# Seven block products in place of eight in the feed-forward down products of a two-block model

## The chip, the cores and the metric

The kernel runs on one core of a Trainium2 chip. The metric is the device time of one launch in microseconds, the median of several runs; the profile is one execution taken by the hardware profiler, with its own span.

## The reference, cut to what matters

A residual stream of 256 tokens by 1024 columns goes through two layers of a first block and two of a second. Each layer is a sum of mixers, then a feed-forward part; only that one is touched here.

```python
# first block, width 2816; the convolution runs over tokens, three taps
y = gelu(conv(h @ ffn_w_gate)) * (h @ ffn_w_up)
x = x + rms_norm(y @ ffn_w_down, post_ffn_g)
# second block, width 4096
m = jnp.square(jax.nn.relu(h @ w_up)) @ w_down
x = x + rmsnorm(m, g_post_mlp)
x = x + jax.nn.sigmoid(x @ w_ple_gate) * (p_i @ w_ple_proj)
```

All operands are float32, x is 256 x 1024, and `w_down` is 2816 x 1024 or 4096 x 1024.

## The kernel before

A float32 product is made of three passes of TensorE (`mm3`, L316): each operand is split into a high part (ScalarE copies it to fp32r, which rounds) and the exact rest (VectorE subtracts the high part), and high by high, high by low and low by high are summed in PSUM.

Weights come as a stream of units that is planned ahead in order of use (`plan`, `plan_ffn` at L1219). A unit is 128x1024 numbers: one load on SP's queue into one of three `raw` buffers, one ScalarE copy (L291) to `wh`, one subtraction (L294) to `wl`, the last one by VectorE or, for a few units next to a norm, by GpSimd. `fetch` (L301) emits units up to two ahead of the one in use; a unit in use keeps one of three slots of converted weights. The order of each engine's instructions is set by the framework's scheduler from the order in which they are written and from slots; in the queues it is fixed.

The feed-forward loop (`first_ffn` L1236, second block from L1646) runs over parts of 256 columns of the hidden width. A part has the up product (in the first block gate and up), 48 matmuls of 256 columns each into a bank of PSUM that `pt` gives in turn out of four (`pd`, `pa`); the nonlinearity; the split of its result `y` (128 x 2 x 256: two tiles of hidden columns, 256 tokens) into `f_h` and `f_l`; and the down product, one part behind the up product, in which the tokens are the stationary operand and the weights move: 2 token tiles x 2 row tiles of the weight x 2 column halves of 512 x 3 passes, 24 matmuls into four banks (`acc`, `pc`). The last three parts' down products (`LAST`) come together at the end, one token tile after the other, so that the norm of the first tile can start.

```python
    def downs(p, n):
        return range(n - LAST, n) if p == n else [p - 1] if 0 < p <= n - LAST else []
```

The functions as they are:

Of the kernel before, what the change touches and what calls it, by code (L numbers as in the profile page):

```python
# [47 lines left out]
# steps of the two token tiles between two products  # L48
# [53 lines left out]
# work slots of a group: (tag, bytes of a partition, count), the smallest that fits is taken  # L102
# [7 lines left out]
# work tiles and banks of the mixers of the second block, in phase one and two  # L110
# [8 lines left out]
# banks of PSUM of a group  # L119
# [11 lines left out]
class K:  # L131
    def __init__(self, ctx, tc, a):
# [17 lines left out]
        self.identb = self.cb[:, 0:128]  # L150
        self.hpi = self.cst.tile([128, 1], F, name="hpi")
# [17 lines left out]
    def acc(self):  # L169
        """banks for the products of phase one, in turn"""  # L170
# [18 lines left out]
    def z(self, shape, name, g=None, dt=F, bufs=None):  # L189
        """work tiles of a group of slots"""  # L190
# [16 lines left out]
    def col_load(self, ap, rows, name):  # L207
        """[rows * 128] contiguous values -> [128, rows] (value r * 128 + p at [p, r])."""
# [9 lines left out]
    def rsq(self, ssq, n, mul, add, name="rs"):  # L218
        """(ssq * mul + add) ** -0.5"""
# [15 lines left out]
    def make(self):  # L235
        """the next of what is made once"""
# [5 lines left out]
    def plan(self, key, ap, rows, nk, c0, n):  # L242
        """a block of columns c0..c0 + n, in units of nk tiles of 128 rows"""
# [3 lines left out]
    def tail(self, kind):  # L247
        """the last units planned are followed by a boundary"""
# [4 lines left out]
    def head(self, kind):  # L253
        """the next units may take those slots as well, when what is before the boundary is done"""
# [8 lines left out]
    def convert(self, i, stack):  # L263
        key, ap, r0, nk, c0, n = self.units[i]
        nc = self.nc
        ld = ap.shape[-1]
        raw = self.wp.tile([128, WMAX], F, name="raw", bufs=RAW)
        # the last units of a product before a boundary have slots of their own
# [13 lines left out]
        # next to a boundary the vector engine has the norms to do, and small pieces let those pass  # L282
# [3 lines left out]
        if near and i >= self.near + first:  # L286
            # the norms of the token tiles go ahead
# [28 lines left out]
    def mm3(self, out, a, b, first, last):  # L316
        """out += (ah + al).T @ (bh + bl)"""
# [6 lines left out]
    def tm(self, xT, *blocks, outs=None):  # L324
        """token-major products: each block (key, tiles of rows in a unit, columns) -> its columns of a bank a token tile"""
# [15 lines left out]
    def fm(self, xT, key, out=None):  # L341
        """feature-major product of 256 columns: [128, 2, 256]"""
# [11 lines left out]
    def fm_early(self, xT, key, banks=("acc", "pc"), out=None):  # L354
        """the same by way of a token-major product, which needs one token tile at a time"""
# [18 lines left out]
    def tsplit(self, src, t, hT, lT, k0, nk):  # L374
        """src [128 tokens, nk * 128] -> transposed and split into hT, lT[:, k0:k0 + nk, token tile t]"""
# [14 lines left out]
    def sum_sq(self, a, b, psum=False):  # L390
        """steps: sum of a ** 2 and b ** 2 over 1024 columns, / 1024 + eps, to the power of -1/2"""
# [19 lines left out]
    def warm(self, x, n):  # L411
        """products of no use: the clock of the tensor engine halves when it rests between two products"""
# [1331 lines left out]
```

## Time and profile before

| | us |
|---|---|
| median of three runs | 1549.75 |
| lowest and highest run | 1545.85, 1552.12 |
| span of the profiled execution | 1548.7 |
| median less that span | 1.05 |
| TensorE busy in the span | 1494.2 |
| VectorE busy | 1007.5 |
| ScalarE busy | 827.9 |
| GpSimd busy | 288.0 |

Busy times of engines overlap. TensorE's matmuls are pipelined and their ends modelled, so its pace is read from starts. A name like L294 is the line of the kernel; `wl<-raw,wh` is what is written and what is read.

### The profile page before, as it was taken

What the parts mean: (1) busy time and instruction counts of PE and PEld (TensorE: products, weight loads), DVE (VectorE), ACT (ScalarE), POOL (GpSimd) and SP (SyncE); (2) the same over time, 40 slices, a digit from 0 to 9 for tenths busy, and PEclk for the clock granted to TensorE, in tenths of its full rate; (3) what the DMA queues carried; (4) which work ended last, traced back from release to release, by engine and by line L of the source; (5) the groups of instructions that cost most, each with busy time, mean ns of one, the idle gap of its engine ahead of it and who ended that gap; (6) DMA issues with size and microseconds to landing.
All of it is one profiled execution on the core that took longest, in us unless ns stands there. A gap on an engine that the chain in (4) does not pass through costs nothing.

```text
span 1548.7 us, 25270 instructions
## 1 busy us (share of the span) xinstructions
PE 1494.2 (96%) x9723; PEld 1337.0 (86%) x9731; DVE 1007.5 (65%) x1737; ACT 827.9 (53%) x1443; POOL 288.0 (19%) x377
## 2 busy tenths in 40 slices
PE   7999999999998999999999999999999999999998
PEld 7978889999896887999978888899977888899996
DVE  6897577556789755656666875554566695654455
ACT  5735456445574534544445674555564575555553
POOL 1554210000255322000033122000014231100010
PEclk9999999999999979999999999999999999999999
DMA  7522246666452213666646343556654543466663
GB/s 236 150 84 83 72 149 189 186 183 198 135 158 79 74 57 111 191 188 181 189 135 191 105 138 116 180 187 190 187 188 135 165 124 109 130 190 188 190 194 109
DMA packets 156422, 234.12 MB, mean 151 GB/s; under 512 B 11700, under 2 KB 118158, under 8 KB 156302
## 3 DMA queue, kind: packets, MB, share of 16 engines
q1 hardware_dynamic: 156302, 232.51, 49.5%
q8 instruction: 76, 1.25, 0.3%
q14 instruction: 44, 0.36, 0.1%
HBM read 231.43 MB, written 1.05 MB: 150 GB/s over the span
## 4 chain that ended last, share of the span: by engine, by line
PE 77%; DVE 12%; ACT 4%; DMA 3%; POOL 2%; issue 2%; SPq 0%; ACTq 0%; DVEq 0%; POOLq 0%
PE acc L322 7%; PE acc L320 7%; PE acc L321 7%; PE pa L320 6%; PE pa L322 6%; PE pa L321 6%; PE pc L320 5%; PE pc L322 5%; PE pc L321 5%; PE pd L322 4%; PE pd L321 4%; PE pd L320 4%; DVE wl L294 3%; DVE gl_r L700 1%; ACT wh L291 1%
## 5 line engine op out<-in xcount | busy, mean ns | idle before, releaser
L294 DVE TENSOR_TENSOR wl<-raw,wh 128x1024 fp32r<-128x1024 f32 (+4 forms) x424 | 485.3, 1152 | 362.8 <-ACT wh L291 361.7
L291 ACT ACTIVATE wh<-raw 128x1024 fp32r<-128x1024 f32 (+4 forms) x420 | 433.2, 1035 | 413.2 <-PE pd L321 100.0
L294 POOL TENSOR_TENSOR wl<-raw,wh 128x1024 fp32r<-128x1024 f32 (+1 forms) x26 | 61.7, 2374 | 647.6 <-ACT wh L291 647.6
L322 PE MATMUL pa<-xTh,wl 128*128 128x256 f32 x512 | 145.5, 284 | 0.0
L320 PE MATMUL pa<-xTh,wh 128*128 128x256 f32 x512 | 145.4, 284 | 0.0
L321 PE MATMUL pa<-xTl,wh 128*128 128x256 f32 x512 | 145.2, 284 | 0.0
L322 PE MATMUL pd<-xTh,wl 128*128 128x256 f32 x432 | 122.4, 283 | 0.5 <-DVE wl L294 0.5
L320 PE MATMUL pd<-xTh,wh 128*128 128x256 f32 x432 | 122.3, 283 | 0.0
L321 PE MATMUL pd<-xTl,wh 128*128 128x256 f32 x432 | 122.2, 283 | 0.0
L320 PEld LDWEIGHTS pa<-xTh,wh 128*128 128x128 f32 x512 | 98.2, 192 | 0.3
L321 PEld LDWEIGHTS pa<-xTl,wh 128*128 128x128 f32 x512 | 98.2, 192 | 0.3
L322 PEld LDWEIGHTS pa<-xTh,wl 128*128 128x128 f32 x512 | 98.1, 192 | 0.2
L320 PEld LDWEIGHTS pd<-xTh,wh 128*128 128x128 f32 x432 | 82.8, 192 | 0.9
L321 PEld LDWEIGHTS pd<-xTl,wh 128*128 128x128 f32 x432 | 82.8, 192 | 0.9
L322 PEld LDWEIGHTS pd<-xTh,wl 128*128 128x128 f32 x432 | 82.8, 192 | 0.8 <-DVE wl L294 0.8
L321 PE MATMUL acc<-wl,f_h 128*128 128x512 f32 x200 | 78.4, 392 | 0.0
L322 PE MATMUL acc<-wh,f_l 128*128 128x512 f32 x200 | 77.3, 390 | 0.6 <-DVE f_l L1259 0.6
L321 PE MATMUL pc<-wl,f_h 128*128 128x512 f32 x200 | 77.8, 389 | 0.0
L322 PE MATMUL pc<-wh,f_l 128*128 128x512 f32 x200 | 77.5, 389 | 0.0
L320 PE MATMUL acc<-wh,xTh 128*128 128x512 f32 (+4 forms) x200 | 71.3, 360 | 1.5 <-ACT xTh L477 1.1
L320 PE MATMUL acc<-wh,f_h 128*128 128x512 f32 x200 | 71.4, 393 | 0.2 <-ACT f_h L1257 0.2
L320 PE MATMUL pc<-wh,f_h 128*128 128x512 f32 x200 | 71.3, 389 | 0.0
(630 smaller groups left out, 3869.8 us busy)
## 6 DMA issues: line engine op xcount, KB each, us to landing
raw<-in_w_in_dram SPq DMA_DIRECT2D x84, 512.0 KB, 3.7
raw<-in_w_mlp_up_dram SPq DMA_DIRECT2D x64, 512.0 KB, 3.8
raw<-in_w_mlp_down_dram SPq DMA_DIRECT2D x64, 512.0 KB, 3.7
raw<-in_ffn_w_gate_dram SPq DMA_DIRECT2D x44, 512.0 KB, 3.8
raw<-in_ffn_w_up_dram SPq DMA_DIRECT2D x44, 512.0 KB, 3.8
raw<-in_ffn_w_down_dram SPq DMA_DIRECT2D x44, 512.0 KB, 3.6
raw<-in_w_out_dram SPq DMA_DIRECT2D x32, 512.0 KB, 3.8
raw<-in_w_ple_gate_dram SPq DMA_DIRECT2D x16, 512.0 KB, 4.3
```

The costliest lines, as they stand in the source:

```text
L291: nc.scalar.activation(h[:, p], raw[:, p], AF.Copy)
L294: e.tensor_tensor(l[:, p], raw[:, p], h[:, p].bitcast(F), OP.subtract)
L320: t.matmul(out, ah, bh, start=first, stop=False, skip_group_check=True)
L321: t.matmul(out, ah, bl, start=False, stop=False, skip_group_check=True)
L322: t.matmul(out, al, bh, start=False, stop=last, skip_group_check=True)
L700: nc.vector.tensor_tensor(R[:, j].rearrange("p h (b s) -> p h b s", s=s), ev[:, ft[j], :, 1][:, None].to_broadcast([128, 2, 128 // s, s]), ...
```

## The change

The down product of a part is a product of 2x2 blocks (two token tiles by two row tiles) with 2x2 blocks (two row tiles by two column halves). For all parts but the last three of a loop it is made of seven block products (Winograd's form) in place of eight. Four sums of token blocks and four of weight blocks are made by GpSimd, each of the operands is then split into high and low part, and the seven products are summed over all these parts in seven banks of PSUM. After the loop the seven banks are combined on ScalarE and VectorE, split once more, and added into the four banks of the last three parts by matmuls with the identity. The eighth bank is all that is left to the up products. In the plan, four units of seven products (two, one, two and two blocks of 128x512) take the place of two units of 128x1024; the loads are the same. They use three slots of their own (`th`, `tl`). In the first block the gate product is copied from PSUM first, and half of the seven products stand between gate and up product. The tables that are made once move from the third part to the last.

Comments removed by the diff and unchanged lines are left out.

```diff
+        self.identr = self.cst.tile([128, 128], FR, name="identr")
+        nc.scalar.activation(self.identr, self.ident, AF.Copy)
...
     def convert(self, i, stack):
+        if nk is None:
+            return self.convert_seven(i, key, ap, r0, c0)
...
     def plan_ffn(self, ups, down, l, width):
-                for key, w in ups:
+                for j, (key, w) in enumerate(ups):
                     self.plan((key, l, p), w, D, 4, p * 256, 256)
-            for q in self.downs(p, n):
-                self.plan((down[0], l, q), down[1][q * 256:q * 256 + 256], 256, 1, 0, D)
+                    for q in self.sevens(p, n):
+                        for which in self.share(j, len(ups)):
+                            self.tails.add(len(self.units))
+                            self.units.append(((down[0], l, q, "s", which), down[1], q * 256, None, which, 0))
+            else:
+                for q in range(n - LAST, n):
+                    self.plan((down[0], l, q), down[1][q * 256:q * 256 + 256], 256, 1, 0, D)
...
+    def sevens(p, n):
+        return [p - 1] if 0 < p <= n - LAST else []
+    def share(j, n):
+        return range(4 * j // n, 4 * (j + 1) // n)
+    def convert_seven(self, i, key, ap, r0, which):
+        nc = self.nc
+        if which == 0:
+            b = []
+            for j in range(2):
+                raw = self.wp.tile([128, WMAX], F, name="raw", bufs=RAW)
+                nc.sync.dma_start(raw, ap[r0 + j * 128:r0 + j * 128 + 128])
+                b += [raw[:, :512], raw[:, 512:]]
+            b11, b12, b21, b22 = b
+            t1, t2, t3, t4 = (self.z([128, 512], "f_t", "d") for _ in range(4))
+            e = nc.gpsimd
+            e.tensor_tensor(t1, b12, b11, OP.subtract)
+            e.tensor_tensor(t3, b22, b12, OP.subtract)
+            e.tensor_tensor(t2, b22, t1, OP.subtract)
+            e.tensor_tensor(t4, b21, t2, OP.subtract)
+            self.sb = [(b11, b21), (b22,), (t1, t3), (t2, t4)]
+        src = self.sb[which]
+        h = self.wp.tile([128, D], FR, name="wh", tag="th", bufs=TAIL)
+        l = self.wp.tile([128, D], FR, name="wl", tag="tl", bufs=TAIL)
+        h, l = (x.rearrange("p (k n) -> p k n", n=512) for x in (h, l))
+        for j, x in enumerate(src):
+            nc.scalar.activation(h[:, j], x, AF.Copy)
+            nc.vector.tensor_tensor(l[:, j], x, h[:, j].bitcast(F), OP.subtract)
+        self.made[i] = (h, l)
+    def seven_banks(self):
+        b = self.bank
+        p2, p3 = b("acc"), b("acc")
+        p4 = b("pc")
+        p1, p5 = b("pd"), b("pd")
+        p6, p7 = b("pa"), b("pa")
+        return [None, p1, p2, p3, p4, p5, p6, p7]
+    def seven_tokens(self, y):
+        nc = self.nc
+        a = self.z([128, 4, 128], "f_s", "G")
+        a11, a12, a21, a22 = y[:, 0, :128], y[:, 1, :128], y[:, 0, 128:], y[:, 1, 128:]
+        e = nc.gpsimd
+        e.tensor_tensor(a[:, 0], a21, a22, OP.add)
+        e.tensor_tensor(a[:, 1], a[:, 0], a11, OP.subtract)
+        e.tensor_tensor(a[:, 2], a11, a21, OP.subtract)
+        e.tensor_tensor(a[:, 3], a12, a[:, 1], OP.subtract)
+        ah, al = (self.z([128, 3, 128], n, g, dt=FR) for n, g in (("f_h", "c"), ("f_l", "a")))
+        sh, sl = (self.z([128, 4, 128], n, "G", dt=FR) for n in ("f_sh", "f_sl"))
+        for h, l, x in ((ah[:, :2], al[:, :2], y[:, :, :128]), (ah[:, 2], al[:, 2], a22), (sh, sl, a)):
+            nc.scalar.activation(h, x, AF.Copy)
+            nc.vector.tensor_tensor(l, x, h.bitcast(F), OP.subtract)
+        pair = lambda h, l, j: (h[:, j], l[:, j])
+        A = lambda j: pair(ah, al, j)
+        S = lambda j: pair(sh, sl, j)
+        return [((1, A(0)), (2, A(1))), ((3, S(3)),), ((5, S(0)), (7, S(2))), ((6, S(1)), (4, A(2)))]
+    def seven(self, P, ops, key, whichs, first, last):
+        for which in whichs:
+            h, l = self.unit(key + ("s", which))
+            for j, (p, a) in enumerate(ops[which]):
+                self.mm3(P[p], a, (h[:, j], l[:, j]), first, last and p in (1, 5, 6, 7))
+    def seven_sums(self, P):
+        nc = self.nc
+        z = lambda: self.z([128, 512], "f_u", "d")
+        c11, u, c21, c12, c22 = z(), z(), z(), z(), z()
+        nc.scalar.activation(c11, P[1], AF.Copy)
+        nc.vector.tensor_tensor(u, c11, P[6], OP.add)
+        nc.vector.tensor_tensor(c21, u, P[7], OP.add)
+        nc.vector.tensor_tensor(c12, u, P[5], OP.add)
+        nc.vector.tensor_tensor(c22, c21, P[5], OP.add)
+        out = []
+        for x in (c11, c12, c21, c22):
...
+            nc.scalar.activation(h, x, AF.Copy)
+            nc.gpsimd.tensor_tensor(l, x, h.bitcast(F), OP.subtract)
+            out.append((h, l))
+        return out
+    def seven_end(self, P, sums):
+        accs = [P[2], P[3], P[4], self.bank("pc")]
+        for i, (b, (h, l)) in enumerate(zip(accs, sums)):
+            self.nc.tensor.matmul(b, self.identr, h, start=i == 3, stop=False, skip_group_check=True)
+            self.nc.tensor.matmul(b, self.identr, l, start=False, stop=False, skip_group_check=True)
+        return [accs[:2], accs[2:]]
+    def up_bank(self, p, n):
+        return self.bank("pc") if p < n - LAST + 2 else self.pt()
     def first_ffn(self, l, xT):
...
-                pg = self.fm(xT, ("gate", l, p), self.pt()) if p else self.fm_early(xT, ("gate", l, p))
+                pg = self.fm(xT, ("gate", l, p), self.up_bank(p, np_)) if p else self.fm_early(xT, ("gate", l, p))
+                x = self.z([128, 2, 256], "f_g", "c")
+                nc.scalar.activation(x, pg, AF.Copy)
...
-                        nc.vector.scalar_tensor_tensor(c[:, f, d:], pg[:, f, :256 - d], w(2 - d, f), c[:, f, d:],
+                        nc.vector.scalar_tensor_tensor(c[:, f, d:], x[:, f, :256 - d], w(2 - d, f), c[:, f, d:],
...
+                if p == 1:
+                    P = self.seven_banks()
+                for q in qs:
+                    self.seven(P, g[q], ("down", l, q), self.share(0, 2), q == 0, q == np_ - LAST - 1)
...
+                if p < np_ - LAST:
+                    g[p] = self.seven_tokens(y)
...
+                for q in qs:
+                    self.seven(P, g[q], ("down", l, q), self.share(1, 2), q == 0, q == np_ - LAST - 1)
+                    del g[q]
+            if p == np_ - LAST:
+                sums = self.seven_sums(P)
+            if p == np_ - 1:
                 self.make()
...
+        accs = self.seven_end(P, sums)
```

The loop of the second block is changed in the same way, with all four units of a part behind the up product.

## Rows read from the trace of the kernel before

**Rows 1.** The page: span, then busy time, share of the span and instructions.
```profile
span 1548.7 us, 25270 instructions
PE 1494.2 (96%) x9723; PEld 1337.0 (86%) x9731; DVE 1007.5 (65%) x1737; ACT 827.9 (53%) x1443; POOL 288.0 (19%) x377
```

**Rows 2.** Windows: stretch, its length, busy time of each engine, granted clock, DMA.
```profile
core 0: us, PE busy (x) PEld busy (x) DVE busy (x) ACT busy (x) POOL busy (x), PEclk, DMA share, GB/s
275.00:350.00 75.00, 75.00 (x541) 71.16 (x540) 45.91 (x55) 35.33 (x44) 0.53 (x1) 1.00 0.63 188
1025.00:1125.00 100.00, 100.00 (x657) 92.05 (x656) 50.21 (x45) 54.44 (x64) 0.00 (x0) 1.00 0.61 190
```

**Rows 3.** Timeline of TensorE, second block: start, duration, engine, line, operation.
```profile
1022.12 0.28 PE L320 MATMUL pd<-xTh,wh 128*128 128x256 f32 x1
...
1027.88 0.40 PE L320 MATMUL acc<-wh,f_h 128*128 128x512 f32 x1
...
1033.34 0.28 PE L320 MATMUL pa<-xTh,wh 128*128 128x256 f32 x1
```

**Rows 4.** Timeline of SP's queue, first block: two successive gate loads.
```profile
276.07 3.21 SPq L281 DMA_DIRECT2D raw<-in_ffn_w_gate_dram  x2
...
293.05 3.21 SPq L281 DMA_DIRECT2D raw<-in_ffn_w_gate_dram  x2
```

**Rows 5.** Timeline of VectorE: back-to-back pairs, and three convolution steps.
```profile
596.56 1.29 DVE L294 TENSOR_TENSOR wl<-raw,wh 128x512 fp32r<-128x512 f32 x2 [6.18 <-ACT wh L291]
...
186.78 2.36 DVE L294 TENSOR_TENSOR wl<-raw,wh 128x1024 fp32r<-128x1024 f32 x2 [2.77 <-ACT wh L291]
...
261.81 1.38 DVE L1250 SCALAR_TENSOR_TENSOR f_c<-pd,f_cw,f_c 128x255 f32<-128x255 f32 x3
```

**Rows 6.** Timeline of GpSimd at three places.
```profile
1132.15 4.76 POOL L294 TENSOR_TENSOR wl<-raw,wh 128x1024 fp32r<-128x1024 f32 x2 [170.38 <-ACT wh L291]
...
386.83 1.39 POOL L294 TENSOR_TENSOR wl<-raw,wh 128x560 fp32r<-128x560 f32 x1 [0.20 <-ACT wh L291]
...
147.71 0.46 POOL L962 TENSOR_TENSOR c_q<-c_q,rp 128x128 f32<-128x128 f32 x1 [0.83 <-DVE rp L961]
```

**Rows 7.** Timeline of GpSimd, then of VectorE, from 204.5 to 209.
```profile
205.71 2.40 POOL L294 TENSOR_TENSOR wl<-raw,wh 128x1024 fp32r<-128x1024 f32 x1 [2.63 <-ACT wh L291]
...
204.66 0.74 DVE L451 SCALAR_TENSOR_TENSOR x<-ny,rs,x 128x512 f32<-128x512 f32 x1
205.32 0.68 DVE L479 TENSOR_TENSOR xTl<-pd,xTh 128x512 fp32r<-128x512 f32 x1
205.92 2.73 DVE L451 SCALAR_TENSOR_TENSOR x<-ny,rs,x 128x512 f32<-128x512 f32 x1
```

**Rows 8.** Timeline of GpSimd, then of VectorE, from 66.7 to 69.7.
```profile
66.71 0.74 POOL L854 TENSOR_TENSOR a_g<-a_g,ngain 128x256 f32<-128x256 f32 x1
67.40 1.45 POOL L704 TENSOR_TENSOR gl_e<-gl_e,b_k 128x128 f32<-128x128 f32 x1
68.81 0.80 POOL L1059 TENSOR_TENSOR d_kd<-d_qk,d_eb 128x256 f32<-128x256 f32 x1
...
67.01 1.52 DVE L294 TENSOR_TENSOR wl<-raw,wh 128x1024 fp32r<-128x1024 f32 x1
68.45 0.68 DVE L1056 TENSOR_TENSOR d_kb<-d_qk,d_beta 128x256 f32<-128x256 f32 x1
```

**Rows 9.** Timeline of ScalarE in the second block's loop.
```profile
1030.20 0.63 ACT L1656 ACTIVATE f_h<-f_y 128x512 fp32r<-128x512 f32 x1
1030.82 1.06 ACT L291 ACTIVATE wh<-raw 128x1024 fp32r<-128x1024 f32 x1
```

**Rows 10.** The page's DMA issues: operation, count, KB each, us to landing.
```profile
raw<-in_w_mlp_down_dram SPq DMA_DIRECT2D x64, 512.0 KB, 3.7
```

**Rows 11.** Timeline of TensorE at a norm; in brackets the idle time before.
```profile
800.01 1.73 PE L472 MATMUL pd<-cf,nxn 128*128 128x128 f32 x8 [2.43 <-DVE nxn L469]
```

**Rows 12.** Windows, the same columns as in rows 2.
```profile
802.00:804.00 2.00, 2.00 (x5) 1.62 (x5) 2.00 (x4) 1.95 (x4) 0.60 (x1) 0.50 0.00 0
```

More of the change, by code (lines that the diff above doesn't have):

```diff
@@ L1231, in downs @@
     @staticmethod
-    def downs(p, n):
-        return range(n - LAST, n) if p == n else [p - 1] if 0 < p <= n - LAST else []
+    def sevens(p, n):
+        return [p - 1] if 0 < p <= n - LAST else []
+    @staticmethod
+    def share(j, n):
[24 more added lines that the diff above has]
+        self.made[i] = (h, l)
@@ new lines, in seven @@
+    def seven(self, P, ops, key, whichs, first, last):
[14 more added lines that the diff above has]
+        for x in (c11, c12, c21, c22):
+            h, l = (self.z([128, 512], n, "G", dt=FR) if n == "f_vh" else self.z([128, 512], n, "N", dt=FR) for n in ("f_vh", "f_vl"))
+            nc.scalar.activation(h, x, AF.Copy)
+            nc.gpsimd.tensor_tensor(l, x, h.bitcast(F), OP.subtract)
+            out.append((h, l))
+        return out
@@ L1241, in first_ffn @@
         for p in range(np_ + 1):
+            qs = self.sevens(p, np_)
             if p < np_:
-                pg = self.fm(xT, ("gate", l, p), self.pt()) if p else self.fm_early(xT, ("gate", l, p))
+                pg = self.fm(xT, ("gate", l, p), self.up_bank(p, np_)) if p else self.fm_early(xT, ("gate", l, p))
+                x = self.z([128, 2, 256], "f_g", "c")
+                nc.scalar.activation(x, pg, AF.Copy)
                 c = self.z([128, 2, 256], "f_c", "c")
@@ L1246, in first_ffn @@
                 for f in range(2):
-                    nc.scalar.activation(c[:, f], pg[:, f], AF.Copy, scale=w(2, f))
+                    nc.scalar.activation(c[:, f], x[:, f], AF.Copy, scale=w(2, f))
                 for f in range(2):
                     for d in (1, 2):
-                        nc.vector.scalar_tensor_tensor(c[:, f, d:], pg[:, f, :256 - d], w(2 - d, f), c[:, f, d:],
+                        nc.vector.scalar_tensor_tensor(c[:, f, d:], x[:, f, :256 - d], w(2 - d, f), c[:, f, d:],
@@ L1251, in first_ffn @@
                                                        op0=OP.mult, op1=OP.add)
                 nc.scalar.activation(c, c, AF.Gelu_apprx_tanh)
-                pu = self.fm(xT, ("up", l, p), self.pt()) if p else self.fm_early(xT, ("up", l, p))
+                if p == 1:
+                    P = self.seven_banks()
+                for q in qs:
+                    self.seven(P, g[q], ("down", l, q), self.share(0, 2), q == 0, q == np_ - LAST - 1)
+                pu = self.fm(xT, ("up", l, p), self.up_bank(p, np_)) if p else self.fm_early(xT, ("up", l, p))
@@ L1265, in first_ffn @@
-            qs = self.downs(p, np_)
-            if qs:
-                self.down(accs, [(g[q][0][:, k], g[q][1][:, k], ("down", l, q, k)) for q in qs for k in range(2)],
-                          p == 1, p == np_)
-            for q in qs:
-                del g[q]
+                if p < np_ - LAST:
+                    g[p] = self.seven_tokens(y)
+                else:
+                    gh = self.z([128, 2, 256], "f_h", "c", dt=FR)
+                    nc.scalar.activation(gh, y, AF.Copy)
+                    gl = self.z([128, 2, 256], "f_l", "a", dt=FR)
+                    nc.vector.tensor_tensor(gl, y, gh.bitcast(F), OP.subtract)
+                    g[p] = (gh, gl)
@@ L1271, in first_ffn @@
+                for q in qs:
[4 more added lines that the diff above has]
+            if p == np_ - 1:
+                self.make()
+        accs = self.seven_end(P, sums)
+        self.down(accs, [(g[q][0][:, k], g[q][1][:, k], ("down", l, q, k)) for q in range(np_ - LAST, np_) for k in range(2)],
+                  False, True)
         return accs
@@ L1647, in second_layer @@
         g, pp = {}, None
-        for p in range(np_ + 1):
-            if p < np_:
-                pu = self.fm(xT, ("2up", l, p), self.pt()) if p > 1 else self.fm_early(xT, ("2up", l, p))
-                r = self.z([128, 2, 256], "f_c", "c")
-                nc.scalar.activation(r, pu, AF.Relu)
-                y = self.z([128, 2, 256], "f_y", "a")
-                nc.scalar.activation(y, r, AF.Square)
+        for p in range(np_):
+            pu = self.fm(xT, ("2up", l, p), self.up_bank(p, np_)) if p > 1 else self.fm_early(xT, ("2up", l, p))
+            r = self.z([128, 2, 256], "f_c", "c")
+            nc.scalar.activation(r, pu, AF.Relu)
+            y = self.z([128, 2, 256], "f_y", "a")
+            nc.scalar.activation(y, r, AF.Square)
+            if p < np_ - LAST:
+                g[p] = self.seven_tokens(y)
+            else:
                 gh = self.z([128, 2, 256], "f_h", "c", dt=FR)
@@ L1660, in second_layer @@
             if p == 1:
-                accs = self.acc4()
-            qs = self.downs(p, np_)
-            if qs:
-                self.down(accs, [(g[q][0][:, k], g[q][1][:, k], ("2down", l, q, k)) for q in qs for k in range(2)],
-                          p == 1, p == np_)
-            for q in qs:
-                del g[q]
+                P = self.seven_banks()
+            for q in self.sevens(p, np_):
+                self.seven(P, g[q], ("2down", l, q), self.share(0, 1), q == 0, q == np_ - LAST - 1)
+                del g[q]
+            if p == np_ - LAST:
+                sums = self.seven_sums(P)
+        accs = self.seven_end(P, sums)
+        self.down(accs, [(g[q][0][:, k], g[q][1][:, k], ("2down", l, q, k)) for q in range(np_ - LAST, np_) for k in range(2)],
+                  False, True)
         ws = [self.unit(("2pp", l, k)) for k in range(2)]
```

8 lines of the change are left out of this document (removed).

## Prediction

> **What bounds the kernel now.** I read the page first: of a span of 1548.7 us TensorE is busy in 1494.2, while GpSimd has only 288.0 us of work [rows 1]. Then the table by windows, for one stretch inside the feed-forward loop of each block: TensorE is busy for the whole of both, at full granted clock, ScalarE and VectorE for about half to six tenths, and GpSimd for nothing but a crumb [rows 2]. The reader is to see that in these loops TensorE alone sets the pace and that GpSimd's queue is empty. The page calls a matmul busy until its modelled end, so the pace is read from starts in the timeline: in the second block one part of the loop starts at 1022.12 and the next at 1033.34, a period of 11.22 us [rows 3]. It holds 48 products of 256 columns (the up product, 1022.12 to 1027.88, so 0.120 us each) and 24 of 512 columns (the down product, 1027.88 to 1033.34, 5.46 us, so 0.2275 us each) and no gap. In the first block the loads come round every 16.98 us [rows 4], that is two up-like products and one down product (2 x 5.76 + 5.46 = 16.98): no gap either.
>
> **What the change takes from TensorE.** A part's down product is eight block products of three passes, 24 matmuls; seven make 21. So 3 x 0.2275 = 0.68 us go in each part that is changed: 8 parts in each of two layers of the first block and 13 in each of two of the second, 42 in all, 126 matmuls, 28.7 us. Added are 8 matmuls with the identity at the end of each of four loops, 32 x 0.2275 = 7.3 us, behind products that keep TensorE busy. Alone this is -21.4 us, and a part would take 10.54 us in the second block and 16.30 in the first.
>
> **What it adds elsewhere.** Per changed part, for the weights: the two halves of a down weight were two tiles of 1024 columns, copied and subtracted in one piece each; now seven blocks of 512 columns are, after four subtractions of 128x512 on GpSimd (t1 to t4). For the tokens: 896 columns are split in three pieces in place of 512 in one, after four GpSimd operations of 128x128. In the first block the gate product is also copied out of PSUM by ScalarE (one copy of 128x512), since the loop has one bank for it now; its four convolution steps then read SBUF only.
>
> VectorE, from pairs that ran back to back [rows 5]: 1.29 / 2 = 0.645 us for 512 columns, 2.36 / 2 = 1.18 for 1024, hence 1.045 ns a column and, on that line, 0.38 for 256 and 0.24 for 128. A part of the second block: 2 x 1.18 (up weights) + 7 x 0.645 + (0.645 + 0.38 + 0.24) = 8.14 us. The first block: 4 x 1.18 + 4.515 + 1.265 + four convolution steps at 0.46 [rows 5] = 12.34 us, and one product with PSUM beside it, 0.65.
>
> GpSimd [rows 6]: 4.76 / 2 = 2.38 us for 1024 columns and 1.39 for 560, 2.13 ns a column, so about 1.29 for 512; 0.46 for 128. Four and four: 5.16 + 1.84 = 7.00 us a part, in loops where it had nothing.
>
> ScalarE in the second block: 0.63 us for a 512-column copy, 1.06 for 1024 [rows 9]; 2 x 1.06 + 7 x 0.63 + 1.2 (relu and square, at that price) + some 1.3 for the tokens = about 9 us, under the 10.54; in the first block 4 x 1.06 + 4.41 + 1.3 and four more at 0.63, 12.5 us under 16.30. Each engine taken by itself fits.
>
> **The pair that doesn't fit.** The rows at 205 us show VectorE and GpSimd side by side [rows 7]. The same VectorE step that takes 0.74 us took 2.73 when it came 0.21 us behind a GpSimd subtraction: it ended at 208.65, 0.54 after GpSimd's end at 208.11, and 0.54 is its 512 columns at 1.045 ns. It had waited for the whole of it. The step between, with an operand in PSUM, took its usual 0.68 although it ended inside the GpSimd instruction. So what excludes GpSimd is VectorE reading two operands of SBUF. Every subtraction raw minus high part does that, and so, after the change, does each convolution step. The two engines then have one budget, and behind a blocked subtraction stand, in VectorE's in-order queue, those of the next up weights, whose low parts TensorE's second or third pass reads.
>
> The sum of durations: 8.14 + 7.00 = 15.14 us in the second block against a period of 11.22; 12.34 + 7.00 = 19.34 in the first against 16.98. The lower bound is that only the columns exclude each other: 6528 x 1.045 + 2560 x 2.13 = 12.28 us in the second block, and 9594 x 1.045 + 5.45 = 15.48 in the first, where TensorE's 16.30 would bind.
>
> Rows 8 put a price between: five operations in turn on the two engines, from 66.71 to 69.61, 2.90 us [rows 8]. By the prices for one (0.74, 1.18, 0.46, 0.38, 0.74) they sum to 3.50, by columns alone to 2.71. Where both queues are full, then, the pair needs 0.83 of the sum: 12.6 us.
>
> The Trainium skill, SBUF — State Buffer, section "Who interferes with whom", has this as a rule: a VectorE instruction with two SBUF inputs and a GpSimd one that reads SBUF contend, and the second to issue is blocked until the first is done. By that rule as it stands, with whole durations and no idle time, the kernel would take about 1549 + 26 x 3.92 + 16 x 2.36 + 7 = 1696 us; by the proportion of rows 8 it would be 1549 + 26 x 1.38 - 16 x 0.68 + 7 = 1581.
>
> I take 15.14 for the second block: a saturated 12.6 needs both queues full, and each VectorE subtraction waits for its own ScalarE copy, each t for a landed load and for the t before it. For the first block I take the middle between TensorE's 16.30 and 19.34, 17.8: its loop has 6 us more, and its 0.65 us product with PSUM leaves the pair free.
>
> **What is near the path besides.** Loads: two of three raw buffers stay taken until the t chain is through. A load lands 3.7 us after issue [rows 10]; 2 x (3.7 + 2.3) for the up weights, an estimated 8 and 12 for the two halves of a down weight (the landing and two or four steps of the t chain), 32 us over three buffers, 10.7 a part: under 15, so not the bound, but every other load queues in order on SP behind it. Banks: up products have one bank; the next up product starts 21 matmuls later (4.8 us; 9 or 12, 2 us or more, in the first block), and the one ScalarE or VectorE read in between, about 0.63 us, is hidden by that. The sums (five ScalarE copies, four VectorE sums and four GpSimd subtractions, 5.2 us on GpSimd) lie under two up products without a down product, 11.5 us; uncovered they would cost 2 us a loop. The one-time tables move to the last up part: nothing, or 2 us once. Identity tile: one copy at the start, nothing.
>
> **Sum.** 26 x (15.14 - 11.22) = +102; 16 x (17.8 - 16.98) = +13; identity products +7; the second block's loops begin with converted units in hand and end without new ones, so half a part's excess less at each of four ends, -8. Together +114: 1549 + 114, about 1663. The page's span is 1 us below the median 1549.75 of the runs, which I use as the start: 1664.
>
> **Rivals.**
> 1. Forecast: the pair of VectorE and GpSimd sets the loop; 1620 to 1710, 1664 likeliest. Chance 0.60.
> 2. The pair interleaves as densely as it can, and only the second block suffers: 26 x 1.06 - 16 x 0.68 + 7 = +24, 1574. For it: rows 8. Against: those five operations were all ready. Chance 0.17.
> 3. Waits come on top of the budget. A unit of seven products has three converted slots for four units, so the fourth unit's copies start when the first unit's products end, with 9 matmuls (2.05 us) of cover; two copies and two subtractions (2 x 0.65 + 2 x 0.645), with a GpSimd instruction of 1.29 let in before each subtraction, are about 4.5 us: 2.5 us bare in each of 42 parts, +105, about 1770. TensorE's clock points the same way: after a gap of 2.43 us [rows 11] it was at 0.50 [rows 12], the 1.2 GHz level. Against: bare time is partly time that the pair uses. Chance 0.15.
> 4. The other side: the pair hides, because GpSimd's instructions fall into VectorE's idle half and are short enough to be let in; TensorE stays the bound and the matmuls saved are the result: 1549.75 - 21.4 = 1528. It decides if the pair's need falls under 10.54 us a part. Rows 7 and 8 speak against: even columns alone ask 12.28. Chance 0.06. Between this and rival 2, no change: 0.02.
>
> **Range and chances.** Low is rival 2, high is rival 3: 1574 to 1770, which leaves out rival 4 and about half of the outer two. A measurement of this kernel can tell 0.5%, 8 us. Faster 0.06, same 0.03, slower 0.91.
>
> **What would show it.** In the profile after: periods of the second block's loop near 15 us (10.5 if rival 4 holds, 12.3 if rival 2) and of the first near 17.8; GpSimd busy near 7 us of each part; VectorE subtractions of 512 columns with a mean well over 0.645 us; TensorE waiting for `wl` of the seven, or for the token parts, in every part; TensorE's busy share in these loops near 0.7 in the second block. I am wrong if the loops hold no TensorE waits although GpSimd works, or if the waits end on loads or PSUM banks instead.

## The result and the profile after

The kernel with seven products takes 1695.88 us (median of four runs, 1689.69 to 1698.44) beside 1550.21 for the kernel before on the same chip: 1.0941 times as long, with an interval of 1.0907 to 1.0975. The profiled execution has a span of 1687.9 us, 139.2 more than that of before.

The page of the changed kernel: span, busy times, the engines' shares of the chain that ended last, and four groups of instructions.

```profile
span 1687.9 us, 26284 instructions
PE 1529.8 (91%) x9637; PEld 1346.7 (80%) x9637; DVE 1325.3 (79%) x2043; ACT 938.9 (56%) x1779; POOL 716.5 (42%) x729
...
PE 43%; DVE 23%; DMA 11%; ACT 9%; issue 7%; POOL 7%; SPq 0%; ACTq 0%; POOLq 0%; DVEq 0%
...
L1278 DVE TENSOR_TENSOR wl<-f_t,wh 128x512 fp32r<-128x512 f32 x168 | 148.3, 912 | 11.5 <-ACT wh L1277 11.5
L1278 DVE TENSOR_TENSOR wl<-raw,wh 128x512 fp32r<-128x512 f32 x126 | 146.0, 1188 | 5.2 <-ACT wh L1277 5.2
...
L1267 POOL TENSOR_TENSOR f_t<-raw 128x512 f32<-128x512 f32 x42 | 65.0, 1547 | 185.9 <-DMA raw<-in_w_mlp_down_dram 79.7
```

GpSimd has gone from 288.0 to 716.5 us, VectorE from 1007.5 to 1325.3 [rows 1]. The shares of the chain before were these:

```profile
PE 77%; DVE 12%; ACT 4%; DMA 3%; POOL 2%; issue 2%; SPq 0%; ACTq 0%; DVEq 0%; POOLq 0%
```

So TensorE's share has fallen from 77% to 43%, and VectorE's has risen from 12% to 23%. The subtraction of 512 columns, 0.645 us where VectorE is alone [rows 5], has a mean of 0.912 or 1.188 here, and a GpSimd sum of 512 columns 1.547 in place of 1.29 [rows 6]. Both are longer where they stand beside each other (experiments 1 and 8).

The windows of before in the same places [rows 2], after (busy time of each engine with its count, then granted clock and load):

```profile
245.00:385.00 140.00, 121.83 (x791) 113.80 (x790) 117.22 (x130) 74.67 (x121) 58.54 (x51) 0.91 0.48 151
1060.00:1200.00 140.00, 122.54 (x733) 104.15 (x732) 134.17 (x125) 81.11 (x144) 103.86 (x84) 0.98 0.49 155
```

In the second block (second row) VectorE is at work, or blocked, for 134.17 of 140 us, so it sets the pace there. In the first block it isn't full, and the granted clock is 0.91. The periods, from SP's queue: two loads of the second block's up weights, two of the first block's gate weights.

```profile
1109.49 6.58 SPq L285 DMA_DIRECT2D raw<-in_w_mlp_up_dram  x2
1122.99 6.56 SPq L285 DMA_DIRECT2D raw<-in_w_mlp_up_dram  x2
...
285.16 2.10 SPq L285 DMA_DIRECT2D raw<-in_ffn_w_gate_dram  x2
305.69 2.10 SPq L285 DMA_DIRECT2D raw<-in_ffn_w_gate_dram  x2
```

One part takes 13.5 us in the second block (11.22 before [rows 3]) and 20.5 in the first (16.98 [rows 4]). Some of TensorE's longest waits (total, times, longest):

```profile
PE pc L324 <- DVE f_y L1372: 35.2, 12, 6.1
PE pc L325 <- DVE wl L1278: 34.6, 23, 2.5
...
PE pa L476 <- DVE nxn L473: 12.5, 6, 6.5
```

The row that is left out, for `nxn` into `pd`, is 14.3 us here and 15.3 before. The second row is the wait that the prediction named, for the low part of a seven's weights. Here is one of them in the second block's timeline (start, duration, engine, line, idle time before and its releaser):

```profile
1151.39 1.40 POOL L1268 TENSOR_TENSOR f_t<-raw 128x512 f32<-128x512 f32 x1 [0.30 <-DMA raw<-in_w_mlp_down_dram]
1151.56 2.79 DVE L1303 TENSOR_TENSOR f_l<-f_y,f_h 128x256 fp32r<-128x256 f32 x2
...
1152.75 1.45 POOL L1269 TENSOR_TENSOR f_t<-raw,f_t 128x512 f32<-128x512 f32 x1
...
1154.28 0.94 DVE L1278 TENSOR_TENSOR wl<-f_t,wh 128x512 fp32r<-128x512 f32 x1
...
1155.14 2.64 DVE L1278 TENSOR_TENSOR wl<-raw,wh 128x512 fp32r<-128x512 f32 x2
1155.27 0.50 PE L325 MATMUL pc<-wl,f_h 128*128 128x512 f32 x1 [1.91 <-DVE wl L1278]
1155.50 1.74 POOL L1270 TENSOR_TENSOR f_t<-raw,f_t 128x512 f32<-128x512 f32 x1
```

Two token splits, of 256 and of 128 columns (the row gives the form of the first), took 2.79 us, 0.63 in experiment 1, while GpSimd ran two weight sums. The low part of a seven's weights was queued behind them (1154.28), and TensorE stood 1.91 us for it. The Trainium skill, SBUF — State Buffer, section "Who interferes with whom", says that of such a pair the second to issue waits; these rows agree.

The wait in the first row was not in the prediction. It is the first block's, and the line is the product `f_y` that empties the only bank of the up products:

```profile
321.25 1.47 POOL L1269 TENSOR_TENSOR f_t<-raw,f_t 128x512 f32<-128x512 f32 x1
321.49 3.48 DVE L1278 TENSOR_TENSOR wl<-raw,wh 128x512 fp32r<-128x512 f32 x2
322.80 1.62 POOL L1270 TENSOR_TENSOR f_t<-raw,f_t 128x512 f32<-128x512 f32 x1
322.83 0.40 PE L324 MATMUL pa<-wh,f_sh 128*128 128x512 f32 x1
...
324.00 0.39 PE L326 MATMUL pc<-wh,f_l 128*128 128x512 f32 x1
...
324.89 1.21 DVE L298 TENSOR_TENSOR wl<-raw,wh 128x1024 fp32r<-128x1024 f32 x1
326.03 0.68 DVE L1372 TENSOR_TENSOR f_y<-f_c,pc 128x512 f32<-128x512 f32 x1
...
326.76 0.39 PE L324 MATMUL pc<-xTh,wh 128*128 128x256 f32 x1 [2.37 <-DVE f_y L1372]
```

Read it upward: TensorE stood 2.37 us for `f_y`, which ran for its usual 0.68; it was queued behind three subtractions, the first two of which took 3.48 us in place of 1.29 beside two GpSimd sums. Between the up product and the next gate product TensorE has only six matmuls, from 322.83 to 324.00: the scheduler has put five of the seven products, 15 matmuls, between gate and up product, where the kernel's text has half of them. After the same gap one part earlier the clock fell to the 1.2 GHz level (the column behind POOL is the granted clock; TensorE had idled from 303.86 to 306.31 and then been busy without a break):

```profile
305.00:306.00 1.00, 0.00 (x0) 0.00 (x0) 1.00 (x2) 0.29 (x1) 0.00 (x0) 1.00 0.14 37
...
309.00:310.00 1.00, 1.00 (x6) 1.00 (x6) 1.00 (x2) 0.32 (x1) 0.65 (x1) 0.50 1.05 362
311.00:312.00 1.00, 1.00 (x11) 1.00 (x10) 0.27 (x2) 0.73 (x1) 0.00 (x0) 1.00 0.09 30
```

From 307.5 to 310.9 matmuls of 256 columns started 0.214 us apart in place of 0.120, which costs 1.5 us. So 16.30 of products, 2.4 of gap and 1.5 of half clock make 20.2 of the 20.5.

The wait for `nxn` into `pa` (3.0 us in all before) is at the norm before the second block's feed-forward part, where the weight sums of the first part already run:

```profile
1018.33 1.74 POOL L1267 TENSOR_TENSOR f_t<-raw 128x512 f32<-128x512 f32 x1
1018.84 3.46 DVE L1278 TENSOR_TENSOR wl<-raw,wh 128x512 fp32r<-128x512 f32 x2
...
1022.22 1.75 DVE L408 SCALAR_TENSOR_TENSOR nsc<-x 128x512 f32<-128x512 f32 x1
...
1027.49 0.90 PE L476 MATMUL pa<-cf,nxn 128*128 128x128 f32 x3 [6.51 <-DVE nxn L473]
```

**Where the 139 us are.** From the first read of a norm (`nsc<-acc`) to the first of the norm behind, the four feed-forward stages took 192.0, 195.7, 189.6 and 189.4 us before and take 229.0, 225.2, 226.8 and 229.4: +37.0, +29.5, +37.2 and +40.0, together 143.7. All else is 4.5 shorter; one stretch of mixers alone is 9 shorter, which has another cause (last section). Eight parts of the first block at +3.5 us (20.5 less 16.98) and the stage's eight identity products (1.8) make 29.8 of its stages; thirteen parts of the second at +2.27 (13.49 less 11.22) and 1.8 make 31.3. What is left over, 7.2, -0.3, 5.9 and 8.7 us, lies at the starts and ends of the loops.

### The profile page after: what moved, and what is told of

Read it like the earlier page. It is cut to its first block, busy times and chain, and to the rows that moved or that the text cites. A ratio compares the mean times of both kernels' runs of the same rounds, so it can differ in the third digit from the quotient of the medians.

```text
span 1687.9 us, 26284 instructions
## 1 busy us (share of the span) xinstructions
PE 1529.8 (91%) x9637; PEld 1346.7 (80%) x9637; DVE 1325.3 (79%) x2043; ACT 938.9 (56%) x1779; POOL 716.5 (42%) x729
## 4 chain that ended last, share of the span: by engine, by line
PE 43%; DVE 23%; DMA 11%; ACT 9%; issue 7%; POOL 7%; SPq 0%; ACTq 0%; POOLq 0%; DVEq 0%
DVE wl L1278 6%; DVE wl L298 6%; PE pc L324 5%; PE pc L325 5%; PE pc L326 5%; PE acc L326 4%; ACT wh L295 3%; PE acc L324 3%; PE acc L325 3%; DMA raw<-in_ffn_w_down_dram 3%; PE pa L324 2%; PE pa L325 2%; PE pa L326 2%; DMA raw<-in_ffn_w_up_dram 2%; DMA raw<-in_w_mlp_up_dram 2%
## 5 line engine op out<-in xcount | busy, mean ns | idle before, releaser
L298 DVE TENSOR_TENSOR wl<-raw,wh 128x1024 fp32r<-128x1024 f32 (+5 forms) x336 | 400.2, 1200 | 177.0 <-ACT wh L295 172.9
L295 ACT ACTIVATE wh<-raw 128x1024 fp32r<-128x1024 f32 (+3 forms) x336 | 343.2, 1026 | 231.9 <-DMA raw<-in_w_mlp_up_dram 43.2
L324 PE MATMUL pc<-xTh,wh 128*128 128x256 f32 x784 | 236.4, 301 | 36.9 <-DVE f_y L1372 35.2
L326 PE MATMUL pc<-xTh,wl 128*128 128x256 f32 x784 | 234.1, 299 | 6.7 <-DVE wl L298 6.7
L325 PE MATMUL pc<-xTl,wh 128*128 128x256 f32 x784 | 234.0, 298 | 0.0
L324 PEld LDWEIGHTS pc<-xTh,wh 128*128 128x128 f32 x784 | 162.5, 207 | 45.7 <-DVE f_y L1372 40.9
L326 PEld LDWEIGHTS pc<-xTh,wl 128*128 128x128 f32 x784 | 162.7, 207 | 8.9 <-DVE wl L298 7.2
L325 PEld LDWEIGHTS pc<-xTl,wh 128*128 128x128 f32 x784 | 163.0, 208 | 2.1
L1278 DVE TENSOR_TENSOR wl<-f_t,wh 128x512 fp32r<-128x512 f32 x168 | 148.3, 912 | 11.5 <-ACT wh L1277 11.5
L1278 DVE TENSOR_TENSOR wl<-raw,wh 128x512 fp32r<-128x512 f32 x126 | 146.0, 1188 | 5.2 <-ACT wh L1277 5.2
```

The lines of the kernel that those rows point to most:

```text
L295: nc.scalar.activation(h[:, p], raw[:, p], AF.Copy)
L298: e.tensor_tensor(l[:, p], raw[:, p], h[:, p].bitcast(F), OP.subtract)
L324: t.matmul(out, ah, bh, start=first, stop=False, skip_group_check=True)
L325: t.matmul(out, ah, bl, start=False, stop=False, skip_group_check=True)
L326: t.matmul(out, al, bh, start=False, stop=last, skip_group_check=True)
L1278: nc.vector.tensor_tensor(l[:, j], x, h[:, j].bitcast(F), OP.subtract)
```

## Experiments

Theory A: VectorE's steps with two operands in SBUF and GpSimd's sums exclude each other. Theory B: the form of the product costs the time by itself (three slots for four units, one bank, later tokens), whoever makes the sums. Ratios are to the kernel before on the same chip.

**1. The same instruction slots, but next to nothing read.** Each weight sum becomes two memsets of 0.525 us and a subtraction of two columns, together about its duration; a token sum becomes one memset and such a subtraction. The sums themselves are left out, so that the products are of other numbers.

```diff
+def write_only(e, out, x, y, op):
+    for _ in range(2 if out.shape[-1] == 512 else 1):
+        e.memset(out, 0.0)
+    e.tensor_tensor(out[:, :2], x[:, :2], y[:, :2], op)
...
-            e.tensor_tensor(t1, b12, b11, OP.subtract)
+            write_only(e, t1, b12, b11, OP.subtract)
...
```

> Each of the eight GpSimd sums of a part is replaced by writing only: one or two memsets of its tile (about as long) and a subtraction of two columns, so that it still waits for the same loads; the sums themselves are left out. Theory A (VectorE's subtractions with two operands in SBUF and GpSimd's reading sums exclude each other): the 512-column subtractions fall back to a mean of 0.65 to 0.70 us, the period of the second block's loop falls from 13.49 us to 10.6 to 11.2, that of the first block's from 20.48 to 16.3 to 17.5, and the time is 1535 to 1580 us. Theory B (the order of the queues, the three raw buffers held by the chain of four sums, and the single PSUM bank of the up products set the periods, whatever GpSimd reads): the periods stay within 1 us of 13.5 and 20.5, and the time is above 1660.

Measured: 1552.41 us, 1.0033 (1.0005 to 1.006). Its page, and its up loads in the second block:

```profile
PE 1485.0 (95%) x9637; PEld 1321.3 (85%) x9637; DVE 1123.8 (72%) x2043; ACT 935.7 (60%) x1779; POOL 612.7 (39%) x1233
...
L1284 DVE TENSOR_TENSOR wl<-raw,wh 128x512 fp32r<-128x512 f32 x126 | 83.0, 686 | 15.9 <-ACT wh L1283 15.6
...
1059.91 3.78 SPq L291 DMA_DIRECT2D raw<-in_w_mlp_up_dram  x2
1070.47 3.80 SPq L291 DMA_DIRECT2D raw<-in_w_mlp_up_dram  x2
1081.25 3.80 SPq L291 DMA_DIRECT2D raw<-in_w_mlp_up_dram  x2
```

GpSimd is busy for 612.7 us, not far from 716.5, yet the subtraction is back at 0.686 and the period at 10.7 us (10.54 predicted for TensorE alone); in the first block it is 16.8 on average (gate loads at 260.13 and 327.17, four parts; 16.30 predicted). So some 144 us of the loss come from what GpSimd reads, and slots and bank by themselves cost 0.1 to 0.5 us a part: theory A. That it isn't the other numbers is shown by experiment 2, where they are right and the subtractions as short. Experiment 1 also shows that the saving is real inside the loops and yet worth nothing over the whole: the time is that of before, where the matmuls saved less the identity products ask for 21.4 us less. Part of where it goes is seen at the start of the second block's loop, in TensorE's timeline of this kernel:

```profile
967.89 1.78 PE L482 MATMUL pa<-cf,nxn 128*128 128x128 f32 x8 [2.28 <-DVE nxn L479]
...
979.81 0.50 PE L330 MATMUL pd<-wh,f_h 128*128 128x512 f32 x1 [2.19 <-ACT f_h L1308]
...
984.34 0.50 PE L330 MATMUL pc<-wh,f_h 128*128 128x512 f32 x1 [2.87 <-ACT wh L1283]
```

7.3 us of waits, where the kernel before has none longer than 0.8 in the same stage. The second token tile of the norm comes later (2.28; why is not shown), and the first seven products come before ScalarE has split the first tokens and copied the second weight unit (2.19 and 2.87). With contention these last two places wait 2.20 and 2.67.

**2. All sums on VectorE.**

```diff
-            e = nc.gpsimd
+            e = nc.vector
...
-        e = nc.gpsimd
+        e = nc.vector
```

> All eight sums of a part go from GpSimd to VectorE, nothing is left out. Theory A: no contention is left, VectorE alone has 8.14 + 4 x 0.645 + 4 x 0.24 = 11.7 us a part in the second block and 12.99 + 3.54 = 16.5 in the first, so the periods are 11.7 to 12.3 and 16.5 to 17.5 and the time is 1560 to 1605 us. Theory B: VectorE's fixed queue only grows longer, what it frees (bank, raw buffers) comes later, and the time is that of the changed kernel or more, 1690 to 1740.

Measured: 1593.66, 1.0283 (1.0237 to 1.0328). Periods of 11.4 us in the second block (1085.83 to 1131.44, four parts) and 17.4 in the first; the subtractions are at 0.69 to 0.70. The same sums cost 102 us less where they add 3.5 us a part to an engine that is already more than half full. Without contention VectorE's own need sets the second block: 8.14 + 4 x 0.645 + 4 x 0.24 = 11.7, a little over what it took.

**3. First block: the bank emptied by ScalarE**, so that the next product needn't wait for VectorE's queue.

```diff
-                nc.vector.tensor_tensor(y, c, pu, OP.mult)
+                nc.scalar.activation(y, pu, AF.Copy)
+                nc.vector.tensor_tensor(y, c, y, OP.mult)
```

> In the first block ScalarE copies the up product out of its bank as soon as it is done, and VectorE multiplies from SBUF; the rest is the changed kernel. Theory C (the first block's 4 us a part over TensorE's 16.30 are the wait for the one bank, 2.4 us, and the half clock that follows it, 1.6 us): the waits of the gate product for the multiplication go, the granted clock in the loop returns to 1.00, the period falls to 17 to 18.5 and the time to 1645 to 1670 us. Theory A alone (the pair's budget sets the first block's period as well): the period stays above 19.5, the waits turn up at converted weights, and the time stays within 15 us of 1696.

Measured: 1678.51, 1.0836 (1.0791 to 1.0882), between the two. The first block's period is 19.3 us (20.5), and the clock over four of its parts 0.96 (0.91). One wait of it, and what stands before it:

```profile
336.22 3.44 DVE L1278 TENSOR_TENSOR wl<-raw,wh 128x512 fp32r<-128x512 f32 x2
336.39 0.63 ACT L1365 ACTIVATE f_c<-f_c 128x512 f32<-128x512 f32 x1 [0.84 <-DVE f_c L1363]
...
337.88 0.58 ACT L1372 ACTIVATE f_y<-pc 128x512 f32<-128x512 f32 x1
...
338.51 0.39 PE L324 MATMUL pc<-xTh,wh 128*128 128x256 f32 x1 [2.08 <-ACT f_y L1372]
```

TensorE now waits for ScalarE's copy, that stands behind the gelu in ScalarE's queue, and the gelu waited for the convolution that GpSimd had held up on VectorE (1.51 us for one step of 0.46). The delay reaches the bank on either road; the emptying by VectorE was one place where it showed. Of the 1.2 us a part that were won, some 1.0 belong to the clock, by an estimate: 0.96 in place of 0.91 over some 20 us.

**4. Seven products in the second block only**, the first block as before.

```diff
-        self.plan_ffn((("gate", a["ffn_w_gate"][l]), ...
+        self.plan_eight((("gate", a["ffn_w_gate"][l]), ...
...
```

> Seven products in the second block only; the first block's loop is that of the kernel before. If the losses are local to each loop, as the profile's stage lengths say (first block +37 and +30 us, second block +37 and +40), the time is 1550 + 77 + about 4 = 1620 to 1640 us, with the second block's period unchanged at 13.5 and the first block's back at 16.98. If the second block inherits part of its loss from the first (load stream, clock), it is below 1610.

Measured: 1626.05, 1.0492 (1.042 to 1.0564). The periods are 16.98 and 13.49, each as in the kernel that it is from; about 78 us of the loss are the second block's and 70 the first's.

**5. The first part's weight sums held behind the norm** in front of the loop.

```diff
...
+                if key[2] == 0:
+                    for ins in self.gates.get("pool", ()):
+                        stack.enter_context(self.tc.issue_after(ins))
...
```

> The changed kernel, but the weight sums of each loop's first part on GpSimd are queued behind the last power of the norm ahead of the loop. Theory A says that in the changed kernel these sums, which are ready early, block VectorE's norm steps at the second block's loops (TensorE waits 6.5 us for the second token tile there, 0.7 us in the kernel before). Then that wait falls to 0.7 to 3.9 us and the time by 5 to 14 us, to 1682 to 1691. Rival: the start of the loop is late for its loads and for token parts converted late; then the wait moves to them and the time stays within 4 us of 1696.

Measured: 1692.15, 1.0937 (1.0902 to 1.0971), not to be told from 1.0941. The longest wait for `nxn` on that line falls from 6.5 to 3.3 us, and all waits for it in that stage, the third, from 6.5 to 4.3. The stage is 1.9 us shorter (the four are 227.6, 225.0, 224.9 and 229.7): that is what the hold is worth at most, and too little to show in the whole time.

**6. Weight sums on VectorE, token sums on GpSimd.**

```diff
             t1, t2, t3, t4 = (self.z([128, 512], "f_t", "d") for _ in range(4))
-            e = nc.gpsimd
+            e = nc.vector
```

> The four weight sums of a part on VectorE, the four token sums (128x128) left on GpSimd; nothing is left out. If the price is the columns that GpSimd reads, only a fifth of them is left, VectorE has 10.7 us a part in the second block and 15.6 in the first, and the kernel lies between writing only and all sums on VectorE: 1560 to 1594 us, periods 10.9 to 11.8 and 16.5 to 17.4. If what counts is that GpSimd works at all between the products (a wait of VectorE and ScalarE for its results), it is slower than all sums on VectorE, 1600 to 1650.

Measured: 1613.45, 1.0443 (1.0409 to 1.0476): 20 us more than with all sums on VectorE. The main expectation was less; the time lies in the range of the other one, 1600 to 1650. The second block has the same period (11.4), the first a longer one (18.4 beside 17.4), and `f_y` is waited for again:

```profile
PE pc L324 <- DVE f_y L1372: 21.1, 13, 4.0
```

Two rows of the second block show that short GpSimd sums are not let in for nothing either; a VectorE step of 512 columns is at 0.68 where GpSimd is idle:

```profile
1068.96 0.90 POOL L1296 TENSOR_TENSOR f_s<-f_s,f_y 128x128 f32<-128x128 f32 x1
...
1069.48 0.94 DVE L1268 TENSOR_TENSOR f_t<-raw 128x512 f32<-128x512 f32 x1
```

Why the first block lost a whole microsecond is not shown: before the `f_y` at 300.04 and at 318.62 GpSimd had been idle for over 14 us, so there it can't have held up VectorE's queue, and between 301 and 307 the granted clock was 0.72.

**7. Weight sums made twice on GpSimd.**

```diff
+            e.tensor_tensor(t1, b12, b11, OP.subtract)
+            e.tensor_tensor(t3, b22, b12, OP.subtract)
+            e.tensor_tensor(t2, b22, t1, OP.subtract)
+            e.tensor_tensor(t4, b21, t2, OP.subtract)
```

> The changed kernel with the four weight sums of a part computed twice on GpSimd, 5.16 us more of reading a part; nothing is left out. Theory A: the pair is the bound, so each part grows by 0.83 to 1.0 of that, 4.3 to 5.2 us, and the time by 42 x 4.3 to 42 x 5.2 us, to 1875 to 1915. Rival: GpSimd's idle time in the loops (a fourth in the second block, half in the first) takes most of it: under 1780.

Measured: 1832.2, 1.1854 (1.1787 to 1.1921), 136 us more than with the sums once, between the expectations. The second block's period is 17.5 us (up loads from 1142.20 to 1212.11, four parts), the first's 23.1. Four more sums cost 4.0 and 2.6 us: 1.0 us each in the second block, 0.77 of their 1.29. The granted clock from 1142 to 1212 is 0.85, but VectorE is busy for 65.95 and GpSimd for 67.00 of these 70 us, so it is the pair that sets the pace. With both queues full, then, a part takes 17.5 of the 20.3 us that its durations sum to, 0.86.

**8. The kernel before with seven idle GpSimd additions** of 128x512 in each part of the second block, read by nobody.

```diff
+                for _ in range(7):
+                    u = self.z([128, 2, 256], "f_u", "d")
+                    nc.gpsimd.tensor_tensor(u, y, y, OP.add)
```

> The kernel before, with seven additions of 128x512 on GpSimd in each part of the second block's loop (9.0 us, both operands the part's own activations, the results unused). Nothing waits for them and TensorE's work is that of before. Theory A: VectorE's subtractions (5.4 us a part) and these exclude each other, 12.4 us a part by columns and 14.4 by durations against a period of 11.22; the loop's period becomes 12.0 to 14.4 and the time 1575 to 1650 us. Rival: without a dependence it stays hidden, 1545 to 1556 us.

Measured: 1568.03, 1.0141 (1.0106 to 1.0176), between the expectations. Groups of its page, and a wait of TensorE:

```profile
L294 DVE TENSOR_TENSOR wl<-raw,wh 128x1024 fp32r<-128x1024 f32 (+4 forms) x424 | 545.8, 1296 | 310.9 <-ACT wh L291 309.4
...
L1657 POOL TENSOR_TENSOR f_u<-f_y 128x512 f32<-128x512 f32 x224 | 354.0, 1616 | 20.6 <-ACT f_y L1654 20.6
...
PE pd L321 <- POOL wl L294: 11.0, 2, 5.5
```

The period is 11.37 us (loads at 1029.98, 1041.34, 1052.71). GpSimd is never idle in the loop, each addition takes 1.62 in place of 1.29, and VectorE's subtractions of 1024 columns 1.2 to 2.1 in place of 1.18; but they are ready early, and TensorE hardly notices. 11.0 of the 22 us are two waits at the loops' ends for a low part that GpSimd itself makes and that stands behind its backlog. By columns alone, one engine after the other, the pair would need 4608 x 1.045 + 3584 x 2.13 ns = 12.4 us a part, and it did all of it in 11.37: the sum of columns, which the prediction took for a lower bound, isn't one. A GpSimd addition kept VectorE from at most (11.37 - 4.82) / 7 = 0.94 us.

**9 and 10. The one-time tables** made behind the first up part of the first loop in place of the last, in the changed kernel and in that of experiment 1.

```diff
-            if p == np_ - 1:
+            if p == 0:
                 self.make()
```

> The changed kernel, but the tables that are made once (bounds and rotary tables) are made behind the first up part of the first block's first loop, in place of behind its last one. Theory A (their move to the last part is what the first loop lost beyond the second, some 7 us: table loads of ScalarE of 1.28 us and a TensorE wait of 2.04 us for a token part with half clock behind it at the loop's end): the first feed-forward stage falls from 228.95 to about 222 to 225 and the time from 1696 to 1686 to 1692. Rival B (the first loop is longer for another reason, its gate and up weights coming in cold, or the tables cost the same wherever they stand): the stage stays within 2 us of 229 and the time within 4 us of 1696.

> The kernel whose sums only write (the four token and four weight sums of each part are memsets and subtractions of 2 columns, so the products are of other numbers), with the one-time tables behind the first up part of the first block's first loop as well. Theory A (in this kernel the matmuls saved, 21.4 us, were eaten by the starts and ends of the loops, and the tables at the end of the first loop are one of these, 5 to 8 us): 1552 falls to 1543 to 1548, the first stage from 197.2 to 190 to 193. Rival B (the tables are not it): within 3 us of 1552.

Measured: 1689.46, 1.0916 (1.0871 to 1.096), and 1556.74, 1.0059 (1.0037 to 1.0081). The first stage went from 229.0 to 224.5 in the one and from 197.4 to 198.6 in the other. In the second the move gained nothing, in the first at most 4.5 us, and its time can't be told from that of the changed kernel. A difference of that size is also within what one stage does from execution to execution: the third stage, which the move doesn't touch, is 226.8 in the changed kernel and 231.7 here. That the tables are what the first loop lost beyond the second is not shown.

## Why the prediction was right, and where its sizes were not

**The mechanism.** The forecast was that VectorE and GpSimd, each able to do its work in time, have one budget between them. Taking the reads away gives the whole loss back with everything else in place (experiment 1); moving the sums gives two thirds of it back (2); making the weight sums twice nearly doubles it (7). Rival 4, that the pair hides, fails by these, though TensorE's part of it was nearly exact: 10.7 and 16.8 us a part in experiment 1 against 10.54 and 16.30. Rival 2, the densest interleaving, fails by the second block's period, 13.49 against 12.28. Rival 3, waits for slots on top of the budget, fails in the second block, where a part takes less than the pair's sum and the same three slots cost 0.1 us without contention; the half clock that it spoke of is there in the first block.

**The second block's term, +102, was too high: 26 x 2.27 = +59.** The step that took whole durations, 15.14 us, is what was mis-sized; the pair needs 13.49, 0.89 of it, between that and the 0.83 of [rows 8]. Experiment 7 points the same way (0.86 for a whole part, 0.77 for a sum that is added).

**The first block's term, +13, was too low: 16 x 3.5 = +56.** The step that failed is the one on banks: the read that empties the one up bank was costed at 0.63 us, hidden by the nine or twelve matmuls between, 2 us or more. Its duration was right (0.68), but it isn't the duration that counts: it waits its turn in VectorE's queue behind subtractions that GpSimd has stretched. Nor are there nine matmuls behind the up product; the scheduler left six, 1.4 us (322.83 to 324.00). By an estimate from their 0.2275 us each, six more would have covered another 1.4 us of the gap of 2.4; no run changed this order. In experiments 1 and 2, with the same six matmuls, the bank with an unblocked VectorE costs 0.5 and 1.1 us over TensorE's 16.30; with blocked steps 4.2. Of these some 1.5 are the half clock that follows the gap.

**Starts and ends, -8, had the wrong sign: about +22** (7.2 - 0.3 + 5.9 + 8.7). The loops were thought to start with units in hand. They start instead with sums that delay a norm, tokens that come late and weights that lie behind ScalarE's activations. Contention is the smaller part of it. Experiment 1, without any, has stages of 197.4, 195.1, 191.6 and 190.8 us; with its own periods and the identity products taken off, its starts and ends cost some 17 us as well, and these eat what seven products save. The waits of TensorE that its trace shows for late tokens, weights and norms, and that before has not, are 7.3 and 5.5 us in the second block's loops and 2.1 in the first block's first one. The split by loops is that of one execution, and what the first loop's 7.2 are made of stays open: the tables, costed at 0 to 2 us, explain at most 4.5.

**The identity products** stand at +7 as costed; none of their waits is among the eleven longest of TensorE.

59 + 56 + 22 + 7 is 144, and 114 was forecast. That it came so near is in part luck: the second block's term was 43 too high and the first block's 43 too low. That whole durations by the rule of the Trainium skill (SBUF — State Buffer, "Who interferes with whom") gave 1696, nearly the time measured, is chance: 3.92 us a part were too much for the second block, 2.36 too little for the first, and in experiment 8 the pair took less than its columns alone.

**What would have beaten the kernel before?** None of these. With all sums on VectorE a part of the second block takes more (11.4 us) than TensorE's old period (11.22), and without any cost for the sums the time is that of before.

## What to carry to other kernels

An engine that is idle is not free: before work goes to GpSimd, add its steps to VectorE's two-operand SBUF steps as one budget, in these loops about 0.8 to 0.9 of their durations, and look at what is queued behind the steps that will be stretched. A short read that frees a PSUM bank is as late as the queue that it stands in, so with one bank count that queue and not the read, and the matmuls that the scheduler really leaves to cover it. And where TensorE sets the pace, a saving of a few per cent in a loop has to be set against what the loop's start costs when its first operands come later.

## What the runs showed that was not expected

- Starts and ends of the loops cost nearly as much without contention, some 17 us in experiment 1, as with it, some 22.
- With GpSimd never idle, VectorE and GpSimd did in 11.37 us what by columns, one after the other, needs 12.4 (experiment 8): the exclusion is not complete.
- The same mixers, between the two feed-forward stages of the first block, took 209.3 us in the profile of before and 200.2 in that of after. In the first the granted clock was 0.72 over the last 37 us, in the second 1.00 over the last 28. Two kernels with the first block as before have 199.2 and 199.3 there, so it belongs to that execution and not to the change.
